# Gates by seven products: where the low parts, the second branch weights and the first output units are parted

## The chip, the cores and the metric

The kernel runs on one core of a Trainium2 chip. The metric is device time of one execution in microseconds (us). The kernel before takes 2453.77 us, the median of three runs (2452.86 to 2455.67).

## The reference

Two layers work on 512 tokens of width 1024, in fp32. Each layer is a SwiGLU feed-forward, a token mixer and a second feed-forward, each followed by a layer norm with a scaled residual. The mixer has three attention branches, `o_a`, `o_b` and `o_c`, each 512 x 512. The change lies in how they are merged:

```python
g = jax.nn.sigmoid(h @ w_gate + b_gate).reshape(B, S, N_BRANCH, D)
merged = g[:, :, 0] * (o_a @ w_br_a) + g[:, :, 1] * (o_b @ w_br_b) + g[:, :, 2] * (o_c @ w_br_c)
return merged @ w_out
```

`h` is 512 x 1024, `w_gate` 1024 x 3072, each `w_br` 512 x 1024 and `w_out` 1024 x 1024.

## The kernel before, in words

**Parts.** TensorE (PE) multiplies in fp32r, and each fp32 operand is split in two parts for it: the high part is a copy made by ScalarE (ACT), the low part is the operand less its high part, made by VectorE (DVE). A product is three matmuls, high by high, high by low and low by high, so the third matmul of a group needs the low part of the weights (`mm3`, L176; `prod`, L1643). `parts` (L1558) issues both halves of a split, ACT's and right behind it DVE's.

**Units and pairs.** The 1024 columns of each branch are eight units of 128. The merged value of branch `br` and unit `d` is a gate (`h` by `w_gate`, contraction 1024) times a branch value (`o` by `w_br`, contraction 512). The first units are made plainly: `plain` (L1657) takes 24 matmuls of 512 columns for a gate. The others are made in pairs of units `d` and `d + 1`, by seven block products for eight: `Two` (L1622) holds the weights of the pair (`rg`, `ru`), `sums` makes four block sums of them on DVE, and `hi` parts four operands: `ug`, `u1`, `u2` and `ud`. `token_sums` (L1602) makes the four sums of token blocks that all pairs share, in two halves `g`; each half is two additions (`back`) and four steps `both`: a subtraction on DVE, a high part on ACT and a low part on DVE.

**The cycle.** `cycle` (L1682) does one pair, the current one (`cur`), while it prepares the next (`nxt`). PE's order in it is seven products of 12 matmuls of 256 columns: two into bank `ga`, two into `pa`, one into `pb`, and two more into `ga`. ACT copies `ga` to `sn` after the second (L1691), and products six and seven then add onto `ga`: the sixth has to wait until `sn` is read. DVE adds the quarters up (L1696 to L1709), ACT makes two gate values by Tanh (L1708 and `gate_ev`, L1462). Behind the seven products come the branch units of the pair, 24 matmuls of 512 columns (`branch`, L1664), whose results DVE multiplies with the gates and adds up in `acc`.

**Order of the cycles.** The pairs are (1,6), (2,2), (2,4), (2,6), (0,2), (0,4) and (0,6). Two of them do two branches, and are called double here: (2,2) does the branch units (2,0) and (2,2), (0,2) does (0,0) and (0,2). They also begin with the split of the next attention output (`split_o`, L1562; its low part is the tile `ol`). Before the first cycle stand eight plain gates and branches, between which the token sums are dealt out two steps at a time (`some`, L1723).

**What sets the order.** The stage is inside `in_order` (L256): PE, ACT, DVE and GpSimd run in the order in which the code issues their instructions. Only the DMA queue of SyncE (SP) is ordered by the planner.

**Buffers.** Raw weights go through three buffers (`wraw`, L126, `raws` at L116). A buffer is free again when both halves of the split have read it. `raw_of` (L1570) loads 512 KB of gate weights with one DMA (L1573), `branch_w` (L1582) 512 KB of branch weights with two (L1586). A pair holds two of the three buffers, `rg` until the low part of `ug`, `ru` until the low part of `ud` (the tile `dl`). The loads for the pair after the next are issued as soon as buffers come free. In a double cycle the second branch's weights are parted into tile `wo`, in the loop at the end of the cycle (L1713), after everything for the next pair but `u2`.

**After the cycles.** `merged` parts the first six units of `acc` in the last cycle, the last two follow (L1766), and `rows_ln` (L287) does the output projection: for each 128 rows of `w_out` a load (`wrows`), a split (L161, L162) and 24 matmuls (L195 to L197) into all eight PSUM banks.

Of the kernel before, what the change touches and what calls it, by code (L numbers as in the profile page):

```python
# [9 lines left out]
F32 = mybir.dt.float32  # L10
F32R = mybir.dt.float32r
BF = mybir.dt.bfloat16
AF = mybir.ActivationFunctionType
OP = mybir.AluOpType
# [4 lines left out]
P = 128  # L19
S, D, F = 512, 1024, 2816  # L20
KD, KF, NB = D // P, F // P, S // P
# [43 lines left out]
def body(tc, a, out, depth=DEPTH):  # L65
    nc = tc.nc
# [7 lines left out]
    wt = pool("wt")  # L74
# [6 lines left out]
    def ps(tag=None, name="ps", shape=(P, 512)):  # L81
        if tag is None:
            tag = PS_ALL[ring[0] % 8]
            ring[0] += 1
        return psp.tile(list(shape), F32, name=name, tag=tag, bufs=PS_TAGS[tag])
# [40 lines left out]
    def wraw():  # L126
        pl, n = raws[0]
        raws.rotate(-1)
        return pl.tile([P, KD, P], F32, name="raw", tag="raw", bufs=n)

    more = K()
# [152 lines left out]
            load(when.pop(0))  # L284
        return wts, {0: lambda: ln.second(NB - 2), 2: lambda: ln.second(NB - 1)}

    def rows_ln(nk, wload, sh, sl, ln, nmain, clear, nxt):  # L287

        accs = [[ps(name="acc") for _ in range(2)] for _ in range(NB)]
        order = in_order()
        for k in range(nmain):
            w = wload(k)
            for tb in range(NB):
                mm_rows(accs, sh, sl, k, tb, w, nk)
        rest = [(k, wload(k)) for k in range(nmain, nk)]
        clear()
        nx.pool = pool("nx", reuse_waits="tile")

        def half(tb, hf):
            for k, w in rest:
                mm_rows(accs, sh, sl, k, tb, w, nk, (hf,))

        wts, pend = norm_tail(accs, half, ln, nxt)
        order.__exit__(None, None, None)
        return wts, pend
# [532 lines left out]
    def mix(l, wts, pend, done_ffn, xap, xa, nxt):  # L840
# [620 lines left out]
        def gate_ev(t, p, br, d):  # L1461
            nc.scalar.activation(t, p, AF.Tanh, scale=0.5, bias=bg[:, br, d:d + 1])  # L1462
# [92 lines left out]
            gate_ev(g1[br], held[br], br, 1)  # L1555
        order = in_order()

        def parts(hi, lo, x):  # L1558
            nc.scalar.activation(hi, x, AF.Copy)
            tt(lo, x, hi.bitcast(F32), op=OP.subtract)  # L1560

        def split_o(br, n=2):  # L1562
            for k in range(0, 4, n):
                c = slice(k, k + n)
                parts(ob[0][:, c], ob[1][:, c], o_t[br][:, c])

        def pair_of(pl):
            return [pl.tile([P, KD, P], F32R, name=n, tag=n, bufs=3 if pl is wt else 2) for n in ("hi", "lo")]
# [10 lines left out]
            parts(*u, r)  # L1579
            return u  # L1580

        def branch_w(br, d, pl):  # L1582
            r = wraw()
            v = wb[br].rearrange("(k p) f -> p k f", p=P)
            for j in range(2):
                nc.sync.dma_start(r[:, 4 * j:4 * j + 4], v[:, :, (d + j) * P:(d + j + 1) * P])  # L1586
            if pl is op:
                u = op.tile([P, 2, KD, P], F32R, name="wo", tag="o2")
                u = u[:, 0], u[:, 1]
            else:  # L1590
                u = pair_of(pl)
            parts(*u, r)
            return u

        def tick(t):
            sums_step(t[:, 0:1] if len(t.shape) == 2 else t[:, 0, 0:1])
# [4 lines left out]

        def token_sums(g):  # L1602
            x = op.tile([P, 4, S], F32, name="x", tag="o1")
            steps = []

            def back(i):
                c, o = slice(4 * i + 2 * g, 4 * i + 2 * g + 2), slice(2 * i, 2 * i + 2)
                tt(x[:, o], xh[:, c].bitcast(F32), xl[:, c].bitcast(F32), op=OP.add)

            p_, q, r_, s_ = x[:, 0:2, H1], x[:, 0:2, H2], x[:, 2:4, H1], x[:, 2:4, H2]  # L1610

            def both(i, o, u, v):
                tt(o, u, v, op=OP.subtract)
                c = slice(2 * g, 2 * g + 2)
                parts(T[i][0][:, c], T[i][1][:, c], o)

            steps += [lambda i=i: back(i) for i in range(2)]
            for z in ((0, p_, q, p_), (2, q, s_, q), (1, s_, s_, p_), (3, r_, r_, s_)):
                steps.append(lambda z=z: both(*z))
            return steps  # L1620

        class Two:  # L1622

# [13 lines left out]
            def hi(u, n):  # L1637
                x = {"ug": u.rg, "u1": u.x1, "u2": u.x2, "ud": u.ru[:, hi4]}[n] if n != "ug" else u.rg
                t = gd if n == "ud" else pair_of(more.pool if n == "ug" else wt)
                setattr(u, n, t)  # L1640
                parts(*t, x)

        def prod(o, w, k0, x, first=True):  # L1643
            for k in range(4):
                hi, lo = w[0][:, k0 + k], w[1][:, k0 + k]
                vh, vl = x[0][:, k], x[1][:, k]
                for i, (wx, vx) in enumerate(((hi, vh), (hi, vl), (lo, vh))):
                    nc.tensor.matmul(o, wx, vx, start=first and k == 0 and i == 0, stop=k == 3 and i == 2,  # L1648
                                     skip_group_check=True)
# [14 lines left out]
        def branch(br, d, w, mid=None):  # L1664
            for j in range(2):
                p = ps(name="brp")
                for k in range(4):
                    mm3(p, w, 4 * j + k, ob[0][:, k], ob[1][:, k], k == 0, k == 3)
                if mid and j == 0:
                    mid()  # L1670
                t, o = g[br, d + j], acc[:, d + j]
                if br == 1:
                    stt(o, t, 1.0, p, op0=OP.add, op1=OP.mult)
                else:
                    stt(t, t, 1.0, p, op0=OP.add, op1=OP.mult)
                    tt(o, o, t, op=OP.add)
            tick(o)
# [1 line left out]
        def temp(n):  # L1679
            return gp.tile([P, S], F32, name=n, tag=n, bufs=2)  # L1680

        def cycle(cur, nxt, brps, end=None):  # L1682
            ga, pa, pb = (ps(name="gate") for _ in range(3))
            if nxt:
                nxt.sums()
            br, d = brps[0]
            w = branch_w(br, d, wt)
            prod(ga[:, H1], cur.ug, 0, XP)
            prod(ga[:, H2], cur.u1, 0, T[0], False)
            sn, v, h = temp("sn"), temp("v"), gate_t(cur.br, cur.d + 1)  # L1690
            nc.scalar.activation(sn, ga, AF.Copy)  # L1691
            if nxt:
                nxt.hi("ug")
            prod(pa[:, H1], cur.u1, 4, T[1])
            prod(pa[:, H2], cur.u2, 0, T[2], False)
            tt(v[:, H1], pa[:, H1], sn[:, H1], op=OP.add)  # L1696
            tt(v[:, H2], pa[:, H2], v[:, H1], op=OP.add)
            tt(h[:, H2], sn[:, H2], v[:, H2], op=OP.add)
            if nxt:
                nxt.hi("u1")  # L1700
            prod(pb[:, H1], cur.ud, 0, T[3])
            tt(h[:, H1], pb[:, H1], v[:, H2], op=OP.add)
            prod(ga[:, H1], cur.ug, 4, XR, False)
            prod(ga[:, H2], cur.u2, 4, XS, False)
            if nxt:
                nxt.hi("ud")
            t = gate_t(cur.br, cur.d)
            nc.scalar.activation(h, h, AF.Tanh, scale=0.5, bias=bg[:, cur.br, cur.d + 1:cur.d + 2])  # L1708
            tt(ga[:, H2], ga[:, H2], v[:, H1], op=OP.add)  # L1709
            gate_ev(t, ga, cur.br, cur.d)  # L1710
            tick(t)
            mid = (lambda: nxt.hi("u2")) if nxt else end
            for i, (br, d) in enumerate(brps):  # L1713
                branch(br, d, w if i == 0 else branch_w(br, d, op), mid)
                mid = None

        wp = [gate_w(2, 1, wt)]
        split_o(1)
# [4 lines left out]
        def some(n):  # L1723
            for _ in range(n):
                steps.pop(0)()
# [17 lines left out]
        some(2)  # L1743
        plain(1, 5, wp[6])
        some(2)
        cur.sums()
        cur.hi("ug")
        branch(1, 4, wp[7])
        for n in ("u1", "u2", "ud"):
            cur.hi(n)  # L1750
        todo = deque([(2, 2), (2, 4), (2, 6), (0, 2), (0, 4), (0, 6)])
        then = Two(*todo.popleft())
        brps = {(1, 6): [(1, 6)], (2, 2): [(2, 0), (2, 2)], (0, 2): [(0, 0), (0, 2)]}

        def merged():
            for d in range(0, 6, 2):
                c = slice(d, d + 2)
                parts(mh[:, c], ml[:, c], acc[:, c])

        while cur:  # L1760
            me = cur.br, cur.d
            if me[1] == 2:
                split_o(me[0])
            cycle(cur, then, brps.get(me, [me]), merged)
            cur, then = then, Two(*todo.popleft()) if todo else None
        for d in (6, 7):  # L1766
            parts(mh[:, d], ml[:, d], acc[:, d])
        order.__exit__(None, None, None)
        gp.release()
        op.release()  # L1770
# [5 lines left out]
        for tb in range(NB):  # L1776
            nc.sync.dma_start(xa2[tb], x_sp[tb * P:(tb + 1) * P, :])
        wts, pend = rows_ln(KD, lambda k: wrows(a["w_out"][l], k), lambda k: mh[:, k], lambda k: ml[:, k], ln,
                            KD - NTAIL, lambda: None, nxt)

        def done():
            nx_close()
# [167 lines left out]
```

## Time and profile before

| What | us |
|---|---|
| median of three runs | 2453.77 |
| the profiled execution | 2453.74 |
| its span, first to last instruction | 2452.0 |
| PE busy | 2418.8 |
| DVE busy | 1947.3 |
| ACT busy | 1229.1 |

The mean granted clock of TensorE in the span is 0.996. The stage of the change stands twice in the span, once in each layer: its first cycle starts at 711.11 and at 1928.64 us, its output projection at 845.54 and at 2061.58 us.

How to read it: times in the rows are microseconds from the span's start. `lo<-raw,hi` is an instruction that writes a tile called `lo` from tiles called `raw` and `hi`; `x2` at the end says that two of them were merged in one row. In square brackets is the idle time of the engine just before, and the instruction that ended it. In the list of waits a row reads: engine, tile and line that waited, what ended the wait, microseconds in total, how often, and the longest. SPq is the DMA queue of SyncE. PEclk is the granted clock as a share of the full one. A matmul's row lasts longer than its share of PE, since the next one starts before it ends.

### The profile page before, as it was taken

How to read it: one execution, taken by the hardware profiler on the slowest of the kernel's cores; microseconds unless marked ns; L12 is line 12 of the kernel's file. 1: busy time of each engine (PE TensorE's matmuls, PEld its weight loads, DVE VectorE, ACT ScalarE, POOL GpSimd, SP SyncE). 2: the span in 40 equal slices, each digit the busy share in tenths (PEclk: the TensorE clock that was granted, in tenths of full speed). 3: DMA queues.
4: the chain of work that ended last, by engine and by line, in shares of the span. 5: the costliest groups of instructions: out<-in, count | busy, mean ns of one | idle time of the engine just before them, and what ended most of it. 6: DMA issues, size and time to landing. Idle time of an engine off the chain costs nothing.

```text
span 2452.0 us, 41947 instructions
## 1 busy us (share of the span) xinstructions
PE 2418.8 (99%) x15952; PEld 2160.7 (88%) x15952; DVE 1947.3 (79%) x3782; ACT 1229.1 (50%) x2336; POOL 487.8 (20%) x684
## 2 busy tenths in 40 slices
PE   9999999999999999999999999999999999999998
PEld 8999887888888889998899998878888888899987
DVE  6899976677677659999879999666776776699997
ACT  4445645576644334445534455456775443344463
POOL 4232402254410001124000004022443100000040
PEclk9999999999999999999999999999999999999999
DMA  7888753676463536787533347446655635333373
GB/s 205 230 223 219 251 170 118 175 166 142 113 180 86 182 119 155 206 208 237 189 110 104 104 139 243 144 141 173 168 134 132 156 95 172 104 95 104 105 242 121
DMA packets 422587, 390.09 MB, mean 159 GB/s; under 512 B 20473, under 2 KB 352393, under 8 KB 422385
## 3 DMA queue, kind: packets, MB, share of 16 engines
q1 hardware_dynamic: 385792, 287.00, 39.4%
q0 software_dynamic: 36592, 100.41, 17.1%
q8 instruction: 126, 2.06, 0.3%
q14 instruction: 77, 0.62, 0.1%
HBM read 360.02 MB, written 93.38 MB: 185 GB/s over the span
## 4 chain that ended last, share of the span: by engine, by line
PE 93%; DVE 4%; issue 1%; ACT 1%; DMA 1%; SPq 0%; DVEq 0%; POOLq 0%; ACTq 0%; POOL 0%
PE acc L331 17%; PE pg L647 17%; PE pu L647 8%; PE pj L182 6%; PE pj L183 6%; PE pj L184 6%; PE pv L647 4%; PE gate L1648 3%; PE sN L1258 2%; PE ptN L1300 1%; PE po L1319 1%; PE brp L184 1%; PE acc L195 1%; PE brp L183 1%; PE brp L182 1%; PE acc L197 1%
## 5 line engine op out<-in xcount | busy, mean ns | idle before, releaser
L162 DVE TENSOR_TENSOR lo<-raw,hi 128x1024 fp32r<-128x1024 f32 (+2 forms) x192 | 223.8, 1183 | 95.9 <-ACT hi L161 95.2
L182 PE MATMUL pj<-xh,hi 128*128 128x512 f32 (+1 forms) x720 | 267.0, 371 | 0.6 <-ACT hi L161 0.6
L161 ACT ACTIVATE hi<-raw 128x1024 fp32r<-128x1024 f32 (+2 forms) x192 | 192.1, 1020 | 130.0 <-PE acc L331 54.6
L184 PE MATMUL pj<-xh,lo 128*128 128x512 f32 (+1 forms) x720 | 254.6, 354 | 0.4 <-DVE lo L162 0.4
L183 PE MATMUL pj<-xl,hi 128*128 128x512 f32 (+1 forms) x720 | 254.4, 353 | 0.0
L647 PE MATMUL pg<-xh,lo 128*128 128x256 f32 x864 | 244.5, 283 | 0.0
L647 PE MATMUL pg<-xl,hi 128*128 128x256 f32 x864 | 244.5, 283 | 0.0
L647 PE MATMUL pg<-xh,hi 128*128 128x256 f32 x864 | 244.5, 283 | 0.0
L331 PE MATMUL acc<-hi,sh 128*128 128x512 f32 x568 | 221.5, 390 | 0.0
L331 PE MATMUL acc<-lo,sh 128*128 128x512 f32 x568 | 221.1, 389 | 0.0
L331 PE MATMUL acc<-hi,sl 128*128 128x512 f32 x568 | 221.0, 389 | 0.0
L352 POOL COPY pace<-sh 64x1 f32<-64x1 f32 x16 | 94.7, 5920 | 473.4 <-ACT sh L592 473.4
L544 DVE TENSOR_TENSOR lo<-ws,hi 128x1024 fp32r<-128x1024 f32 x144 | 175.2, 1217 | 0.0
L647 PEld LDWEIGHTS pg<-xh,hi 128*128 128x128 f32 x864 | 165.9, 192 | 0.2
L647 PEld LDWEIGHTS pg<-xl,hi 128*128 128x128 f32 x864 | 165.9, 192 | 0.2
L647 PEld LDWEIGHTS pg<-xh,lo 128*128 128x128 f32 x864 | 165.9, 192 | 0.0
L647 PE MATMUL pu<-th,hi 128*128 128x256 f32 x576 | 163.0, 283 | 0.0
L647 PE MATMUL pu<-tl,hi 128*128 128x256 f32 x576 | 163.0, 283 | 0.0
L647 PE MATMUL pu<-th,lo 128*128 128x256 f32 x576 | 163.0, 283 | 0.0
L184 PEld LDWEIGHTS pj<-xh,lo 128*128 128x128 f32 x720 | 136.1, 189 | 20.2 <-DVE lo L162 0.6
L541 ACT ACTIVATE hi<-ws 128x1024 fp32r<-128x1024 f32 x144 | 144.0, 1048 | 16.9 <-DVE ws L526 15.3
L182 PEld LDWEIGHTS pj<-xh,hi 128*128 128x128 f32 x720 | 136.4, 189 | 16.3 <-issue 3.7
(418 smaller groups left out, 7068.0 us busy)
## 6 DMA issues: line engine op xcount, KB each, us to landing
raw<-in_ffn_w_dram SPq DMA_DIRECT2D x228, 512.0 KB, 4.6
ts<-in_ffn_w_dram POOLq DMA_DIRECT2D x72, 768.0 KB, 7.5
raw<-in_w_in_dram SPq DMA_DIRECT2D x56, 512.0 KB, 4.0
raw<-ts SPq DMA_DIRECT2D x52, 512.0 KB, 3.9
raw<-in_w_gate_dram SPq DMA_DIRECT2D x48, 512.0 KB, 4.8
ts<-ts POOLq DMA_DIRECT2D x24, 768.0 KB, 7.8
x_sp<-xa POOLq DMA_DIRECT2D x24, 512.0 KB, 6.2
ks<-hl SPq DMA_DIRECT2D x96, 128.0 KB, 2.4
```

What stands on the lines that cost most here:

```text
L161: nc.scalar.activation(hi[:, c], raw[:, c], AF.Copy)
L162: nc.vector.tensor_tensor(lo[:, c], raw[:, c], hi[:, c].bitcast(F32), op=OP.subtract)
L182: nc.tensor.matmul(o, hi[:, k], vh, start=first, stop=False)
L183: nc.tensor.matmul(o, hi[:, k], vl, start=False, stop=False)
L184: nc.tensor.matmul(o, lo[:, k], vh, start=False, stop=last)
L331: nc.tensor.matmul(o, xx[:, t], ww[:, c], start=first and i == 0, stop=last and i == 2)
L352: nc.gpsimd.tensor_copy(pace[0:64], sp(min(p + 1, NS - 1))[0][0:64, 0, 0:1].bitcast(F32))
L541: nc.scalar.activation(t[0], x, AF.Copy)
L544: nc.vector.tensor_tensor(t[1], x, t[0].bitcast(F32), op=OP.subtract)
L647: nc.tensor.matmul(o, wx, vx, start=first and k == 0 and i == 0, stop=k == 3 and i == 2, skip_group_check=True)
L1258: nc.tensor.matmul(o[:, 0:nb].rearrange("p k b j -> p (k b j)"), q, kx[:, 2 * b0:2 * (b0 + nb)].rearrange("p a b -> p (a b)"), start=i == ...
L1648: nc.tensor.matmul(o, wx, vx, start=first and k == 0 and i == 0, stop=k == 3 and i == 2, skip_group_check=True)
```

## The change

Splits are issued in two steps. A new helper `high` issues ACT's half and returns a function that issues DVE's half later. `parts` is the two together. With it:

- In `token_sums`, the low part of each step is issued one step later, after the next subtraction. A half has seven steps for six, and one more `some(2)` stands before the first pair.
- The first pair's four high parts are issued together, then its four low parts, and the branch (1,4) behind them.
- In `cycle`, the weights of all its branches are loaded and their high parts issued at the head, ahead of `ug` and `sn`. The low parts follow `sn`. The high parts of `ug`, `u1`, `ud` and `u2` are issued one product sooner than their low parts; `u2` stands ahead of the second gate value.
- In the last cycle, the first unit of `w_out` is loaded and parted at the head, the high parts of the first six units of `acc` ahead of the gate value and their low parts behind it. Units 1 and 2 of `w_out` are parted right after the last branch, and `rows_ln` takes these three as `ready`.

```diff
-    def rows_ln(nk, wload, sh, sl, ln, nmain, clear, nxt):
+    def rows_ln(nk, wload, sh, sl, ln, nmain, clear, nxt, ready=()):
...
-            w = wload(k)
+            w = ready[k] if k < len(ready) else wload(k)
...
+        def high(hi, lo, x):
+            nc.scalar.activation(hi, x, AF.Copy)
+            return lambda: tt(lo, x, hi.bitcast(F32), op=OP.subtract)
+
         def parts(hi, lo, x):
-            nc.scalar.activation(hi, x, AF.Copy)
-            tt(lo, x, hi.bitcast(F32), op=OP.subtract)
+            high(hi, lo, x)()
...
-        def branch_w(br, d, pl):
+        def branch_w(br, d, pl, now=True):
...
-            parts(*u, r)
+            lo = high(*u, r)
+            if not now:
+                return u, lo
+            lo()
             return u
...
-                parts(T[i][0][:, c], T[i][1][:, c], o)
+                los.append(high(T[i][0][:, c], T[i][1][:, c], o))
+                if len(los) > 1:
+                    los.pop(0)()
...
-            return steps
+            return steps + [lambda: los.pop(0)()]
...
-                parts(*t, x)
+                return high(*t, x)
...
-        def cycle(cur, nxt, brps, end=None):
+        def cycle(cur, nxt, brps, end):
             ga, pa, pb = (ps(name="gate") for _ in range(3))
+            none = lambda: None
+            hi = nxt.hi if nxt else lambda n: none
             if nxt:
                 nxt.sums()
-            br, d = brps[0]
-            w = branch_w(br, d, wt)
+            ws = [branch_w(br, d, op if i else wt, False) for i, (br, d) in enumerate(brps)]
+            lo = hi("ug")
             prod(ga[:, H1], cur.ug, 0, XP)
             prod(ga[:, H2], cur.u1, 0, T[0], False)
             sn, v, h = temp("sn"), temp("v"), gate_t(cur.br, cur.d + 1)
             nc.scalar.activation(sn, ga, AF.Copy)
-            if nxt:
-                nxt.hi("ug")
+            for _, f in ws:
+                f()
+            lo()
             prod(pa[:, H1], cur.u1, 4, T[1])
+            lo = hi("u1")
             prod(pa[:, H2], cur.u2, 0, T[2], False)
...
-            if nxt:
-                nxt.hi("u1")
+            lo()
             prod(pb[:, H1], cur.ud, 0, T[3])
+            lo = hi("ud")
             tt(h[:, H1], pb[:, H1], v[:, H2], op=OP.add)
             prod(ga[:, H1], cur.ug, 4, XR, False)
+            lo()
+            nc.scalar.activation(h, h, AF.Tanh, scale=0.5, bias=bg[:, cur.br, cur.d + 1:cur.d + 2])
             prod(ga[:, H2], cur.u2, 4, XS, False)
-            if nxt:
-                nxt.hi("ud")
             t = gate_t(cur.br, cur.d)
-            nc.scalar.activation(h, h, AF.Tanh, scale=0.5, bias=bg[:, cur.br, cur.d + 1:cur.d + 2])
+            lo = hi("u2") if nxt else end()
             tt(ga[:, H2], ga[:, H2], v[:, H1], op=OP.add)
             gate_ev(t, ga, cur.br, cur.d)
+            lo()
             tick(t)
-            mid = (lambda: nxt.hi("u2")) if nxt else end
-            for i, (br, d) in enumerate(brps):
-                branch(br, d, w if i == 0 else branch_w(br, d, op), mid)
-                mid = None
+            for (br, d), (w, _) in zip(brps, ws):
+                branch(br, d, w)
...
         some(2)
+        some(2)
         cur.sums()
-        cur.hi("ug")
+        los = [cur.hi(n) for n in ("ug", "u1", "u2", "ud")]
+        for f in los:
+            f()
         branch(1, 4, wp[7])
-        for n in ("u1", "u2", "ud"):
-            cur.hi(n)
...
+        def out_w(k):
+            r = wraw()
+            nc.sync.dma_start(r.rearrange("p k f -> p (k f)"), wo[k * P:(k + 1) * P, :])
+            u = pair_of(wt if k else more.pool)
+            ws_.append(u)
+            return high(*u, r)
+
         def merged():
-            for d in range(0, 6, 2):
-                c = slice(d, d + 2)
-                parts(mh[:, c], ml[:, c], acc[:, c])
+            los = [high(mh[:, c], ml[:, c], acc[:, c]) for c in (slice(d, d + 2) for d in range(0, 6, 2))]
+            return lambda: [f() for f in los]
...
+            if not then:
+                out_w(0)()
             cycle(cur, then, brps.get(me, [me]), merged)
             cur, then = then, Two(*todo.popleft()) if todo else None
+        los = [out_w(k) for k in (1, 2)]
         for d in (6, 7):
-            parts(mh[:, d], ml[:, d], acc[:, d])
+            los.append(high(mh[:, d], ml[:, d], acc[:, d]))
+        for f in los:
+            f()
+        more.n = 3
```

More of the change, by code (lines that the diff above doesn't have):

```diff
@@ L1603, in token_sums @@
             x = op.tile([P, 4, S], F32, name="x", tag="o1")
-            steps = []
+            steps, los = [], []
             def back(i):
@@ L1753, in mix @@
         brps = {(1, 6): [(1, 6)], (2, 2): [(2, 0), (2, 2)], (0, 2): [(0, 0), (0, 2)]}
+        wo, ws_ = a["w_out"][l], []
+        def out_w(k):
[4 more added lines that the diff above has]
+            return high(*u, r)
         def merged():
-            for d in range(0, 6, 2):
-                c = slice(d, d + 2)
-                parts(mh[:, c], ml[:, c], acc[:, c])
+            los = [high(mh[:, c], ml[:, c], acc[:, c]) for c in (slice(d, d + 2) for d in range(0, 6, 2))]
+            return lambda: [f() for f in los]
         while cur:
@@ L1778, in mix @@
         wts, pend = rows_ln(KD, lambda k: wrows(a["w_out"][l], k), lambda k: mh[:, k], lambda k: ml[:, k], ln,
-                            KD - NTAIL, lambda: None, nxt)
+                            KD - NTAIL, lambda: None, nxt, ws_)
         def done():
```

## The prediction

> **What bounds the kernel now.** I read the page first. The profiled execution took 2453.74 us, of which its span is 2452.0; the other 1.74 us lie outside and I keep them. The runs shown have the median 2453.77, so a sum made on the profiled execution may be read as one on the median.
>
> ```profile
> PE 2418.8 (99%) x15952; PEld 2160.7 (88%) x15952; DVE 1947.3 (79%) x3782; ACT 1229.1 (50%) x2336; POOL 487.8 (20%) x684
> ```
>
> TensorE is the bound, and the change removes and adds no matmul. It can only move the time in which PE stands still. So the second view is the list of waits, for PE alone:
>
> ```profile
> PE brp L184 <- DVE wo L1560: 12.0, 4, 3.0
> PE gate L1648 <- DVE lo L1560: 4.9, 3, 2.1
> PE gate L1648 <- ACT sn L1691: 1.8, 2, 1.3
> ...
> PE acc L195 <- DVE t L1675: 0.7, 2, 0.4
> ```
>
> These rows of both layers are what the change can reach: 12.0 + 4.9 + 1.8 + 0.7 = 19.4 us. Third, the windows view puts a price on each place, since a wait also costs what follows it. The columns are the stretch, its length, five engines with their busy time, the granted clock, the share of DMA, GB/s.
>
> ```profile
> core 0: us, PE busy (x) PEld busy (x) DVE busy (x) ACT busy (x) POOL busy (x), PEclk, DMA share, GB/s
> 711.11:726.00 14.89, 10.85 (x85) 10.23 (x84) 12.26 (x17) 6.59 (x8) 0.00 (x0) 1.00 0.32 93
> 731.47:741.54 10.07, 10.07 (x85) 10.07 (x84) 9.90 (x15) 5.37 (x7) 0.00 (x0) 1.00 0.14 42
> 726.00:731.47 5.47, 5.47 (x26) 4.51 (x25) 3.63 (x6) 3.18 (x4) 0.00 (x0) 1.00 0.79 230
> 741.54:757.47 15.93, 12.89 (x50) 10.11 (x49) 8.69 (x12) 4.37 (x5) 0.00 (x0) 0.89 0.39 110
> 798.63:814.47 15.84, 12.89 (x51) 10.12 (x50) 8.60 (x12) 4.37 (x5) 0.00 (x0) 0.89 0.38 110
> 1928.64:1943.59 14.95, 12.28 (x85) 11.59 (x84) 12.26 (x17) 6.59 (x8) 0.00 (x0) 0.89 0.34 95
> 1959.13:1975.06 15.93, 12.89 (x51) 10.09 (x50) 8.70 (x12) 4.36 (x5) 0.00 (x0) 0.89 0.37 110
> 2016.20:2030.51 14.31, 11.36 (x51) 8.95 (x50) 8.60 (x12) 4.37 (x5) 0.00 (x0) 1.00 0.42 122
> 845.54:852.00 6.46, 6.03 (x26) 4.35 (x24) 6.42 (x9) 2.61 (x4) 0.00 (x0) 1.00 0.70 210
> ```
>
> An undisturbed set of seven products takes 10.07 us and an undisturbed branch of 24 matmuls 5.47. Against these, cycle (1,6) loses 14.89 - 10.07 = 4.82 and 14.95 - 10.07 = 4.88. The two double branches, (2,0) with (2,2) and (0,0) with (0,2), should take 10.94; they lose 4.99, 4.90, 4.99 and 3.37, together 18.25. The last of these four ran at clock 1.00, the others at 0.89: a half-clock stretch behind the wait costs 4.96 (their mean) - 3.37 = 1.6 us. The first unit of the output projection loses 6.46 - 5.47 = 1.0, in each layer. All other cycles have no gap (731.47:741.54 is busy throughout), so what the change does in them is worth nothing unless it breaks them.
>
> **The second branch weights, moved to the head of the double cycles.** This is the largest term, and I take it from the queues. ACT and DVE work in the order in which the kernel is written, and three raw buffers are all there are. At the head of cycle (0,2) two of them hold the gate weights of the next pair, the third the weights of (0,0). The second branch's load needs a buffer; the rows show when it gets one (DVE, then the SP queue, then the landings of all branch loads of the first layer's cycles), what ACT does meanwhile, and when the sixth product starts on PE:
>
> ```profile
> 792.12 1.05 ACT L1559 ACTIVATE hi<-raw 128x1024 fp32r<-128x1024 f32 x1
> ```
> ```profile
> 794.89 2.35 DVE L1560 TENSOR_TENSOR lo<-raw,hi 128x1024 fp32r<-128x1024 f32 x2
> ```
> ```profile
> 796.14 0.92 SPq L1586 DMA_DIRECT2D raw<-in_w_br_a_dram  x2
> ```
> ```profile
> DMA to landing us min/median/max: 2.7/3.3/4.9
> ```
> ```profile
> 795.75 0.28 PE L1648 MATMUL gate<-xh,hi 128*128 128x256 f32 x1
> ```
>
> The load is issued at 796.14, just when the first of the two low parts of 794.89 (half of 2.35) is done. That frees the buffer of (0,0). The change does not free it earlier: its low part still stands behind the four sums on DVE. What changes is who waits. Today ACT parts `ug` at 792.12 and the second weights only after `u2`, at the end of the cycle, long after they have landed. In the new order the high part of the second weights stands ahead of `ug` and of `sn` on ACT. So ACT must wait for the load: second half issued at about 796.6 (half of 0.92 later), landing 3.3 after that at 799.9; high part 0.97 (721.43 to 722.40 in the rows below), 800.85; `ug`, 801.8; `sn`, 0.58, 802.4. The sixth product writes on the bank that `sn` reads and was due at 795.75. It starts 0.05 after that: a wait of about 6.7 us. What is queued behind on ACT is everything else of the cycle, and DVE waits as well, since the low part of the second weights stands ahead of that of `ug`.
>
> That this is how the queues behave is shown in cycle (1,6) of before, where the same thing happens on a smaller scale:
>
> ```profile
> 721.43 1.06 ACT L1559 ACTIVATE hi<-raw 128x1024 fp32r<-128x1024 f32 x1 [7.31 <-DMA raw<-in_w_br_b_dram]
> 722.40 0.58 ACT L1691 ACTIVATE sn<-gate 128x512 f32<-128x512 f32 x1
> ```
> ```profile
> 723.03 0.39 PE L1648 MATMUL gate<-xh,hi 128*128 128x256 f32 x1 [1.27 <-ACT sn L1691]
> ```
>
> A high part waits 7.31 us for its load, `sn` runs right behind it, and PE resumes 0.05 after `sn`.
>
> Cycle (2,2) is the same with one shift. Here DVE comes to the head late today:
>
> ```profile
> 730.68 1.23 DVE L1560 TENSOR_TENSOR lo<-ws,hi 128x1024 fp32r<-128x1024 f32 x1 [1.76 <-ACT hi L1559]
> 731.82 1.28 DVE L1673 SCALAR_TENSOR_TENSOR acc<-t,brp 128x512 f32<-128x512 f32 x2
> 733.02 2.36 DVE L1560 TENSOR_TENSOR ol<-o,oh 128x1024 fp32r<-128x1024 f32 x2
> ```
>
> With the low part of `u2` moved ahead of the branch, the last accumulation can start some 0.2 after PE leaves the branch at 731.47 (an estimate: PE's last matmul ends after the next has started) and take half of 1.28. The `ol` row moves from 733.02 to about 732.3, and the whole chain by 0.7: a wait of 6.0.
>
> To each wait I add what row 2016.20 shows beyond the bare wait (3.37 against 3.0, so 0.4) and one half-clock stretch (1.6). That is 6.0 + 6.7 + 2 x 2.0 = 16.7 per layer, 33.4 in both. The four waits for `wo` end, since its low part is done long before the second branch; they gave 18.25. Net +15.15 us. The landing is the open size: 2.7 or 4.9 instead of 3.3 make it 2.4 less or 6.4 more over four cycles; I take the median, since no gate load will run beside it.
>
> [...]
>
> **Cycle (1,6).** Product one waits for the low part of `ug`. Its chain starts when ACT has evacuated gate (1,5) and runs through the last token sum:
>
> ```profile
> 707.11 0.69 DVE L1560 TENSOR_TENSOR mm<-x,mm 128x512 fp32r<-128x512 f32 x1 [2.15 <-ACT mm L1559]
> 707.72 0.69 DVE L1613 TENSOR_TENSOR x<-x 128x512 f32<-128x512 f32 x1
> 709.10 0.69 DVE L1560 TENSOR_TENSOR mm<-x,mm 128x512 fp32r<-128x512 f32 x1 [0.70 <-ACT mm L1559]
> ```
>
> One step behind means that three high parts, not two, follow the evacuation. DVE then does a low part at 707.11, the last sum at 707.72, the low part that was put off at 708.33, and the last one when its high part is there, at 709.10 as today. The 0.7 us hole is filled with work that used to lie earlier. `ug` and product one gain nothing.
>
> The four low parts of the first pair then stand together, the two accumulations of branch (1,4) behind them; that is 1.2 us sooner for `u1` and `ud`.
>
> ```profile
> 715.98 0.39 PE L1648 MATMUL gate<-mm,lo 128*128 128x256 f32 x1 [0.63 <-DVE lo L1560]
> ...
> 721.48 0.28 PE L1648 MATMUL gate<-mm,dl 128*128 128x256 f32 x1
> ```
> ```profile
> 716.97 0.69 DVE L1560 TENSOR_TENSOR dl<-raw,dh 128x512 fp32r<-128x512 f32 x1
> ```
> ```profile
> 717.69 0.92 SPq L1586 DMA_DIRECT2D raw<-in_w_br_b_dram  x2
> ```
>
> The wait of 0.63 (0.9 with the restart, an estimate) goes. But PE only comes to product six sooner, at 720.7 for 721.6, and that one waits for `sn`. The branch load is issued once `dl` has freed a buffer, so 1.2 us sooner; the high part of `ug`, now ahead of `sn`, takes 0.95 of it back. Product six starts 0.25 sooner: 0.5 us in both layers. Its wait grows to about 2.1, the length at which one of today's two (14.89 at clock 1.00, 14.95 at 0.89) had a half-clock stretch. Before, that stretch was hidden under the next wait; now nothing is behind it. Bounds 0 and 2 x 1.6; I take one, +1.6.
>
> **The last cycle.**
>
> ```profile
> 851.20 0.50 PE L195 MATMUL acc<-hi,mm 128*128 128x512 f32 x1 [0.36 <-DVE t L1675]
> ```
> ```profile
> 840.20 2.96 ACT L161 ACTIVATE hi<-raw 128x1024 fp32r<-128x1024 f32 x3 [0.68 <-ACT hi L161]
> 843.06 0.67 ACT L1462 ACTIVATE t<-gate,bgate 128x512 f32<-128x512 f32 x1
> ```
>
> Today units of the output weights are parted ahead of the last gate value, three of them just before it, so that it comes at 843.06, and their low parts keep DVE from the last branch's result, for which the output projection then waits. In the new order unit 0 is parted at the head of the cycle, where DVE is free of pair sums, and units 1 and 2 after the branch; unit 1 is wanted 5.4 us later. The 1.0 us per layer goes: -2.0, bounds 0 and -2.0. Unit 0's load stands ahead of the last branch's on SP, which then goes out one buffer release later, 1.2 us (half of 2.35); loads for a single cycle go out most of a cycle before they are wanted, so that covers it.
>
> **Edits at nothing.** In single cycles the low parts are issued one step later and `u2` before the gate value: DVE no longer waits for ACT (1.76 in the row at 730.68), but PE has no gap there. The gate value comes 0.97 later and is wanted only when PE ends the first branch unit, 2.7 after product seven. The next pair's loads slip by about 5 us in a double cycle; they are wanted a whole cycle later. POOL's copies and weight sums feed the next stage.
>
> **Sum.** +15.15 - 0.5 + 1.6 - 2.0 = +14.25 on 2453.74: 2468.0. Lowest: short landings (-2.4), no clock loss in (1,6) (-1.6), and half-clock stretches of which half falls into the wait (-0.8 x 4): 2460.8. Highest: long landings, 2474.4.
>
> **Rivals.** First, the intended outcome, and faster: the second weights have landed when ACT comes to them. The four waits of 18.25 go without a new one, with -0.5 and -2.0: 2433. It decides if the load is issued 3.8 us (0.46 + 3.3) before 792.12, where ACT now goes on after the first weights, so by 788.3. For it speaks that the first branch's load is always early. Against it stands the SP queue, which holds the second load back for the low part of the first:
>
> ```profile
> SPq L1586 <- DVE lo L1560: 8.0, 1, 8.0
> ```
>
> It would need a fourth buffer, or another order on ACT than the written one; chance 0.10. Second, no change that can be measured: the new waits are there but come without clock loss and with landings of 2.7. That is 5.4 + 6.1 + 0.8 per layer, 24.6 for 18.25, less 2.5: +3.85, 2457.6. Half-clock stretches followed three waits of about 3 us out of four, and these are twice as long: 0.10. Third, a longer half clock. Row 741.54 lacks 0.11 of the clock in 15.93 us, so some 3.5 us ran at half. A wait of over 6 us is longer than such a stretch; the clock would be halved within it, and if PE's return in the middle of a stretch does not count, a second one follows, at up to 3.2 for 1.6 each time. With all four: 2468.0 + 6.4 = 2474.4. 0.12. [...] The forecast keeps 0.68.
>
> **How the numbers follow.** About 0.2% (4.9 us) is what a measurement of this kernel can tell from no change. Forecast and third rival lie above +0.2%: slower 0.80. Second: same 0.10. First: faster 0.10. The range 2454 to 2474.5 holds the forecast's 2460.8 to 2474.4, the third up to its full price and the upper part of the second; it leaves out the first and the tails.
>
> **What would show it.** Right: in the waits of PE, `brp <- DVE wo` is gone, and `gate <- ACT sn` has grown from 1.8 to about 2 x (6.0 + 6.7) plus 2 x 2.1 us; in ACT, a high part in both double cycles that waits 7 to 9 us for a branch load, `ug` and `sn` behind it; SP issuing the second load right after the first low part; the 2.1 before product one unchanged; no wait for `t` at L1675 under the output projection. Wrong: the second load issued before that low part, or `sn` at 3 us into the double cycles as now; then the first rival holds. If the waits are there and the time is lower than forecast, the clock column of the double cycles tells it.

## The result and the profile after

The changed kernel takes 2468.93 us (median of six runs, 2467.5 to 2470.85) against 2453.37 for the kernel before in the same session (2452.86 to 2455.67). The ratio is 1.0062, 95% interval 1.0049 to 1.0075: slower by 0.6%, with 2468.0 forecast. The profiled execution took 2468.07, its span is 2466.4.

The engines' line of the page, and below it the waits of PE (total, times, longest):

```profile
PE 2423.0 (98%) x15952; PEld 2168.5 (88%) x15952; DVE 1949.1 (79%) x3782; ACT 1228.2 (50%) x2336; POOL 487.4 (20%) x684
```
```profile
PE gate L1656 <- ACT sn L1701: 25.1, 6, 6.6
PE gate L1656 <- DVE lo L1560: 4.3, 2, 2.1
```

The number of matmuls is the same. `brp <- DVE wo` (12.0) and `acc <- DVE t` (0.7) are gone from the list, and the wait for `sn` has gone from 1.8 to 25.1 us. The windows view prices it; the rows are cycle (1,6), then products and branches of the double cycles (2,2) and (0,2), then the first output unit, in the first layer and in the second:

```profile
710.61:725.18 14.57, 12.06 (x85) 11.65 (x84) 13.33 (x19) 6.59 (x8) 0.00 (x0) 0.88 0.42 118
1935.93:1950.41 14.48, 12.08 (x86) 11.67 (x84) 13.33 (x19) 6.59 (x8) 0.00 (x0) 0.88 0.41 116
730.65:748.48 17.83, 12.05 (x85) 11.85 (x84) 12.21 (x16) 6.68 (x8) 0.00 (x0) 0.81 0.30 87
748.48:759.57 11.09, 11.09 (x51) 9.03 (x50) 5.80 (x8) 3.65 (x4) 0.00 (x0) 1.00 0.18 51
790.65:809.55 18.90, 12.34 (x85) 12.13 (x84) 12.89 (x17) 6.68 (x8) 0.00 (x0) 0.82 0.29 82
809.55:820.63 11.08, 11.08 (x51) 9.03 (x50) 5.80 (x8) 3.65 (x4) 0.00 (x0) 1.00 0.17 50
1955.88:1973.84 17.96, 12.07 (x86) 11.87 (x85) 12.20 (x16) 6.68 (x8) 0.00 (x0) 0.81 0.28 84
2016.00:2034.77 18.77, 12.49 (x86) 12.28 (x85) 12.90 (x17) 6.69 (x8) 0.00 (x0) 0.82 0.29 84
851.71:857.15 5.44, 5.44 (x25) 4.50 (x24) 5.37 (x8) 2.30 (x3) 0.00 (x0) 1.00 0.47 140
2076.94:2082.38 5.44, 5.44 (x25) 4.50 (x24) 5.37 (x8) 2.29 (x3) 0.00 (x0) 1.00 0.47 131
```

Seven undisturbed products take 10.07 us, so the products of the four double cycles lose 7.76, 8.83, 7.89 and 8.70, and each double branch 0.14: 33.7 us for the 18.25 of before. Cycle (1,6) loses 0.8 less than before in the two layers together, the first output unit 2.0 less. That makes +15.5 - 0.8 - 2.0 = +12.7 of the 14.4 by which the span has grown.

In cycle (0,2) the cause stands in four queues, DVE, SP, ACT and PE:

```profile
796.99 1.22 DVE L1560 TENSOR_TENSOR lo<-raw,hi 128x1024 fp32r<-128x1024 f32 x1
```
```profile
798.23 0.92 SPq L1589 DMA_DIRECT2D raw<-in_w_br_a_dram  x2
```
```profile
802.03 1.06 ACT L1559 ACTIVATE wo<-raw 128x1024 fp32r<-128x1024 f32 x1 [9.16 <-DMA raw<-in_w_br_a_dram]
802.99 1.04 ACT L1559 ACTIVATE hi<-raw 128x1024 fp32r<-128x1024 f32 x1
803.93 0.58 ACT L1701 ACTIVATE sn<-gate 128x512 f32<-128x512 f32 x1
```
```profile
804.57 0.58 PE L1656 MATMUL gate<-xh,hi 128*128 128x256 f32 x1 [6.56 <-ACT sn L1701]
```

The low part of the first branch weights ends at 798.2 and frees the third buffer; the load goes out at once, 7.58 us into the cycle, as in the kernel before (796.14 - 788.56). ACT waits 9.16 us for it with `ug` and `sn` behind, and PE waits for `sn`.

### The profile page after: what moved, and what is told of

Same layout as the page of the kernel before. It is cut to its first block, busy times and chain, and to the rows that moved or that the text cites. A ratio compares the mean times of both kernels' runs of the same rounds, so it can differ in the third digit from the quotient of the medians.

```text
span 2466.4 us, 41973 instructions
## 1 busy us (share of the span) xinstructions
PE 2423.0 (98%) x15952; PEld 2168.5 (88%) x15952; DVE 1949.1 (79%) x3782; ACT 1228.2 (50%) x2336; POOL 487.4 (20%) x684
## 4 chain that ended last, share of the span: by engine, by line
PE 96%; DVE 2%; DMA 1%; ACT 1%; issue 1%; POOL 0%; SPq 0%; DVEq 0%; POOLq 0%; ACTq 0%
PE acc L331 17%; PE pg L647 17%; PE pu L647 8%; PE pj L182 6%; PE pj L183 6%; PE pj L184 5%; PE gate L1656 5%; PE pv L647 4%; PE brp L184 2%; PE brp L182 2%; PE brp L183 2%; PE sN L1258 2%; PE ptN L1300 1%; PE po L1319 1%; PE acc L196 1%; PE acc L197 1%
## 5 line engine op out<-in xcount | busy, mean ns | idle before, releaser
L162 DVE TENSOR_TENSOR lo<-raw,hi 128x1024 fp32r<-128x1024 f32 (+2 forms) x186 | 217.2, 1186 | 88.9 <-ACT hi L161 87.9
L161 ACT ACTIVATE hi<-raw 128x1024 fp32r<-128x1024 f32 (+2 forms) x186 | 185.8, 1019 | 131.3 <-PE acc L331 52.9
```

The costliest lines, as they stand in the source:

```text
L161: nc.scalar.activation(hi[:, c], raw[:, c], AF.Copy)
L162: nc.vector.tensor_tensor(lo[:, c], raw[:, c], hi[:, c].bitcast(F32), op=OP.subtract)
```

## The experiments

Each time is a median with the ratio to the kernel before from the same session, in which that took 2453.0 to 2454.1.

**The second branch weights back at the loop's end.**

```diff
-            ws = [branch_w(br, d, op if i else wt, False) for i, (br, d) in enumerate(brps)]
+            ws = [branch_w(*brps[0], wt, False)]
...
-            for (br, d), (w, _) in zip(brps, ws):
-                branch(br, d, w)
+            for i, (br, d) in enumerate(brps):
+                branch(br, d, branch_w(br, d, op) if i else ws[0][0])
```

> The kernel after, with one part undone: the second branch weights of the double cycles are loaded and parted in the loop at the cycle's end again. Theory (the order on ACT at the head of the double cycles costs the time): the four waits of product six for sn of 6 to 6.7 us go, the four waits for wo of 3.0 come back, and what the rest of the change gains stays, 2.5 us: 2451 us, 1.5 either way. Rival (the other edits cost it, by disturbing the single cycles or cycle (1,6)): at least half of the 15 us stays, 2461 to 2469.

Measured 2443.18 us, ratio 0.9956 (0.9942 to 0.9970): 26 us faster than the kernel after, and 8 us better than the theory's number. The four waits for `wo` came back, but shorter, and without any loss of clock (waits of PE; then the first double branch):

```profile
PE brp L184 <- DVE wo L1560: 8.7, 4, 2.2
```
```profile
741.28:754.81 13.53, 11.35 (x50) 8.95 (x49) 8.04 (x12) 4.71 (x6) 0.00 (x0) 1.00 0.41 116
```

All four take 13.5, at clock 1.00, a loss of 2.6 each: 10.4 for 18.25. DVE shows why. In the kernel before the second weights are parted behind all four parts of the next pair, `u2` too. The low part of `u2` comes late there, and the four accumulating steps stand in a row between it and the low part of `wo` (three of them shown), for which PE waits:

```profile
745.62 1.23 DVE L1560 TENSOR_TENSOR lo<-ws,hi 128x1024 fp32r<-128x1024 f32 x1 [1.70 <-ACT hi L1559]
746.76 0.68 DVE L1675 SCALAR_TENSOR_TENSOR g<-g,brp 128x512 f32<-128x512 f32 x1
747.47 0.69 DVE L1676 TENSOR_TENSOR acc<-acc,g 128x512 f32<-128x512 f32 x1
748.08 0.68 DVE L1675 SCALAR_TENSOR_TENSOR g<-g,brp 128x512 f32<-128x512 f32 x1
...
749.41 1.22 DVE L1560 TENSOR_TENSOR wo<-raw,wo 128x1024 fp32r<-128x1024 f32 x1
```

In this experiment it comes 0.86 after the gate sum, DVE has caught up, and is itself waiting when PE ends the second unit:

```profile
743.76 1.22 DVE L1560 TENSOR_TENSOR lo<-ws,hi 128x1024 fp32r<-128x1024 f32 x1 [0.86 <-ACT hi L1559]
...
746.95 0.69 DVE L1683 SCALAR_TENSOR_TENSOR g<-g,brp 128x512 f32<-128x512 f32 x1 [0.64 <-PE brp L184]
...
748.28 1.22 DVE L1560 TENSOR_TENSOR wo<-raw,wo 128x1024 fp32r<-128x1024 f32 x1
```

From the end of the products (741.54 before, 741.28 here) to the low part of `wo` it is 7.9 us before and 7.0 here.

So the rest of the change is worth more than the 2.5 us that the prediction gave it, and the place of the second weights costs 26.

**The order within the cycle, alone.** In the kernel before: high parts one product ahead of their low parts (so `ug` ahead of `sn`), the low part of the first branch weights behind `sn`, `u2` ahead of the gate value, and nothing else of the change. Its last lines:

```diff
...
+            lo = hi("u2")
             tt(ga[:, H2], ga[:, H2], v[:, H1], op=OP.add)
             gate_ev(t, ga, cur.br, cur.d)
+            lo()
             tick(t)
-            mid = (lambda: nxt.hi("u2")) if nxt else end
...
```

> The kernel before, with one part of the change alone: the order of the high and low parts within a cycle (one product sooner, u2 ahead of the gate value). Second branch weights, token sums, first pair and output units are as before. Theory from the run with the second weights at the loop's end: the four waits for wo fall from 3.1 to 2.3 us because the low part of u2 no longer stands between the accumulations, and fewer half-clock stretches follow: 7.5 us less, 2446.5 us, 2444 to 2450. Rival, the prediction's own sum (this order is worth nothing as long as the wait for wo stands): 2453 to 2455.

Measured 2448.99 us, 0.9983 (0.9975 to 0.9992). The waits for `wo` are 8.7 in all, as above, and the branches 13.53 again, 7.9 us less. But cycle (1,6) got longer, 16.01 and 17.13 for 14.89 and 14.95, which takes 3.3 back:

```profile
1924.45:1941.58 17.13, 12.24 (x85) 11.63 (x84) 14.65 (x21) 7.16 (x9) 0.00 (x0) 0.90 0.42 120
```

So the order is worth 4 us by itself. With the token sums and the first pair as in the change, (1,6) takes 14.5 to 14.7 (the experiment above and the kernel after), and the 3.3 us are not lost; which of these two edits does it was not separated.

**The head of the cycle, alone.** The kernel before, with only the prediction's main term:

```diff
-            br, d = brps[0]
-            w = branch_w(br, d, wt)
+            ws = [branch_w(br, d, op if i else wt) for i, (br, d) in enumerate(brps)]
...
-                branch(br, d, w if i == 0 else branch_w(br, d, op), mid)
+                branch(br, d, ws[i], mid)
```

> The kernel before, with one part of the change alone: the weights of both branches of a double cycle loaded and parted at its head. Theory, the main term of the prediction: the four waits for wo go (18.25 us) and four waits for sn come; ug stands behind sn here, so each is 0.95 shorter than in the kernel after, and DVE comes 0.7 later to the head of cycle (2,2): 5.7 us each and 2.0 for restart and clock, 31 us. Net +12.5: 2466 us, 2463 to 2469. Rival (without the other edits the load lands in time, or the waits hide each other): within 3 us of the kernel before, 2450 to 2456.

Measured 2467.44 us, 1.0057 (1.0044 to 1.0069). Nearly the whole loss is in this one edit, 14.0 us of 15.6. The waits of PE for `sn`:

```profile
PE gate L1648 <- ACT sn L1690: 23.4, 6, 5.6
```

**A fourth buffer.** The kernel after, with the second weights loaded into two gate tiles that are free by then, each half parted by itself:

```diff
+        def second_w(br, d):
+            v = wb[br].rearrange("(k p) f -> p k f", p=P)
+            u = op.tile([P, 2, KD, P], F32R, name="wo", tag="o2")
+            los = []
+            for j, r in enumerate((g1[1], gates0[1])):
+                r = r.rearrange("p (k f) -> p k f", k=4)
+                nc.sync.dma_start(r, v[:, :, (d + j) * P:(d + j + 1) * P])
+                los.append(high(u[:, 0, 4 * j:4 * j + 4], u[:, 1, 4 * j:4 * j + 4], r))
+            return (u[:, 0], u[:, 1]), lambda: [f() for f in los]
...
-            ws = [branch_w(br, d, op if i else wt, False) for i, (br, d) in enumerate(brps)]
+            ws = [second_w(br, d) if i else branch_w(br, d, wt, False) for i, (br, d) in enumerate(brps)]
```

> The kernel after, with the second branch weights loaded into two tiles that are free by then, so that the load does not wait for the low part of the first branch weights; the place on ACT at the head of the cycle stays. The two halves are parted one by one, two instructions more on ACT and on DVE in each double cycle. Theory (ACT waits because the load is issued only when a raw buffer is free): PE's four waits for sn in the double cycles fall to under 1 us, no wait for wo comes, 2435 us, 2432 to 2440. Rival (the four high and low parts at the head are too much work for ACT and DVE, wherever the load is): the waits stay above 3 us each and the time above 2455.

Measured 2435.11 us, 0.9922 (0.9910 to 0.9935). The order on ACT is that of the kernel after; only the load no longer waits for a buffer, and in cycle (0,2) nothing on ACT waits for it:

```profile
785.67 1.14 ACT L1559 ACTIVATE wo<-g 128x512 fp32r<-128x512 f32 x2
786.71 1.05 ACT L1559 ACTIVATE hi<-raw 128x1024 fp32r<-128x1024 f32 x1
787.66 0.57 ACT L1711 ACTIVATE sn<-gate 128x512 f32<-128x512 f32 x1
```

The work at the head is not too much for ACT and DVE; the buffer was what held it.

**`sn` first.** The kernel after with one line moved; the load is as late as before:

```diff
-            ws = [branch_w(br, d, op if i else wt, False) for i, (br, d) in enumerate(brps)]
+            ws = [branch_w(*brps[0], wt, False)]
...
             nc.scalar.activation(sn, ga, AF.Copy)
+            ws += [branch_w(br, d, op, False) for br, d in brps[1:]]
```

> The kernel after, with one line moved: load and high part of the second branch weights are issued right behind sn, not ahead of ug and sn. The load goes out as late as before and ACT still waits for it, but sn no longer stands behind it. Theory (the time is lost because PE's product six hangs on sn): no wait for sn in the double cycles, the rest of the cycle on DVE and ACT comes 5 to 6 us late and is just in time for the next cycle: 2434 us, 2432 to 2438. Rival (the late load delays the gates and the next pair all the same): a wait of 2 us or more turns up at the branches or at the next cycle's first products, 2442 or more.

Measured 2433.77 us, 0.9920 (0.9906 to 0.9934). ACT still stands still for 6.79 us in cycle (2,2), now behind `sn`, and PE does not notice (ACT; then the seven products of (2,2)):

```profile
734.14 0.60 ACT L1701 ACTIVATE sn<-gate 128x512 f32<-128x512 f32 x1
741.52 1.06 ACT L1559 ACTIVATE wo<-raw 128x1024 fp32r<-128x1024 f32 x1 [6.79 <-DMA raw<-in_w_br_c_dram]
```
```profile
731.07:741.14 10.07, 10.07 (x85) 10.07 (x84) 6.59 (x8) 3.47 (x4) 0.00 (x0) 1.00 0.19 54
```

So the late load costs nothing in itself. What costs is that the one instruction for which PE waits stands behind it.

**The second weights behind `u2` and the gate value.** No extra buffer, load and parts just ahead of the first branch:

```diff
-            ws = [branch_w(br, d, op if i else wt, False) for i, (br, d) in enumerate(brps)]
+            ws = [branch_w(*brps[0], wt, False)]
...
             gate_ev(t, ga, cur.br, cur.d)
+            late = [branch_w(br, d, op, False) for br, d in brps[1:]]
             lo()
+            for _, f in late:
+                f()
             tick(t)
-            for (br, d), (w, _) in zip(brps, ws):
+            for (br, d), (w, _) in zip(brps, ws + late):
```

> The kernel after, with load and high part of the second branch weights issued after u2 and the gate value, and the low part behind that of u2, ahead of the first branch; no extra buffer. Theory (only the place on ACT and DVE matters): sn comes at its old time, the low part of wo is done before the first branch is half through, so neither wait is there: 2433 us, 2430 to 2438. Rival (a second branch's weights can't be ready in the cycle without waiting, the load or the low part is late wherever it stands): waits for wo of 2 us or more stay in the double cycles, 2445 to 2455.

Measured 2433.87 us, 0.9918 (0.9904 to 0.9931); in the double cycles neither wait is there. Its two cycles (1,6) show something else, one with a half-clock stretch and one without (clock 0.88 and 1.00):

```profile
711.00:725.54 14.54, 12.07 (x85) 11.66 (x84) 13.38 (x19) 6.59 (x8) 0.00 (x0) 0.88 0.43 119
1917.16:1931.72 14.56, 10.57 (x85) 10.16 (x84) 13.32 (x19) 6.59 (x8) 0.00 (x0) 1.00 0.43 120
```

They take the same time. The slower PE only comes later to product six, which has to wait for `sn` anyway: 0.4 us in the first, 1.8 us in the second.

**The wait filled with work.** The kernel after, with 24 matmuls more in each double cycle, ahead of product six:

```diff
+            if len(brps) > 1:
+                dm = ps(name="gate")
+                for i in range(24):
+                    nc.tensor.matmul(dm, cur.ug[0][:, i % 8], xh[:, i % 8], start=i == 0, stop=i == 23)
             prod(ga[:, H1], cur.ug, 4, XR, False)
```

> The kernel after, with 24 extra matmuls of 512 columns (128 x 512, 24 x 0.23 = 5.4 us, their result is not used) on PE ahead of product six in the double cycles: PE is busy in most of the wait for sn, and product six starts when it would have. Theory (the wait costs its own length, and a half clock behind it about 1.6 to 2.0 us more): product six starts no later, the clock stays at 1.00 in the double cycles, so 4 x 1.7 us less: 2462 us, 2460 to 2464. Rival (the clock takes no part, the wait is all): no change, 2468 to 2470.

Measured 2460.96 us, 1.0033 (1.0021 to 1.0044): 96 matmuls more, 8 us less. The products of (0,2) take 16.83 with the extra work, 18.90 without:

```profile
788.75:805.58 16.83, 15.80 (x109) 14.49 (x108) 11.64 (x15) 5.96 (x7) 0.00 (x0) 1.00 0.22 65
```

The other three double cycles gain 1.8, 1.9 and 1.7; all four have clock 1.00, for 0.81 to 0.82 in the kernel after. Product six starts within 0.2 us of its place in the kernel after in three of the four and 0.5 later in the fourth; from there to the branch PE takes 3.0 us for 4.7 to 5.1. So these 7.5 us of 33.7 are the clock's share of the loss.

**The first output units, alone**, in the kernel before:

```diff
+            if not then:
+                out_w(0)()
...
+        los = [out_w(k) for k in (1, 2)]
```

> The kernel before, with one part of the change alone: the first three units of the output weights parted in and right behind the last cycle. Theory: the wait for the last branch's result ahead of the output projection goes, 1.0 us in each layer: 2451.8 us, 2450.5 to 2453.5. Rival (the wait only moves, to unit 1 or to the last units of acc): 2453.8, within 1 us of the kernel before.

Measured 2450.63 us, 0.9990 (0.9981 to 0.9999). The first output unit takes 5.44 for 6.46 in both layers; the further 1.4 us are within the interval.

```profile
843.87:849.31 5.44, 5.44 (x25) 4.50 (x24) 5.37 (x7) 3.56 (x5) 0.00 (x0) 1.00 0.00 0
```

**The first pair ahead of gate (1,5).** The experiment with the second weights behind `u2`, and besides:

```diff
-        plain(1, 5, wp[6])
         some(2)
         some(2)
         cur.sums()
         los = [cur.hi(n) for n in ("ug", "u1", "u2", "ud")]
         for f in los:
             f()
+        plain(1, 5, wp[6])
         branch(1, 4, wp[7])
```

> The kernel with the second weights behind u2 and the gate value (2433.9 us), and besides the last four token-sum steps and the whole preparation of the first pair issued ahead of the gate unit (1,5), so that ACT and DVE do not wait for its evacuation first. Theory (both waits of cycle (1,6) hang on that evacuation, by which ACT stands idle for 4.2 us): product one no longer waits 2.1 us, the branch load goes out some 4 us sooner and sn is not late, 4.5 us in each layer: 2425 us, 2424 to 2428. Rival (the first pair is limited by the work of DVE or by its loads): at least half of the waits stays, 2429 to 2434.

Measured 2425.30 us (four runs, 2424.24 to 2432.18), 0.9894 (0.9879 to 0.9910), the fastest version of all: 27.7 us below the kernel before. ACT parts `ug` in the time in which it used to wait for gate (1,5), and evacuates that gate later; cycle (1,6) then loses 0.6 us in the first layer and 0.5 in the second (ACT; windows):

```profile
704.49 1.05 ACT L1559 ACTIVATE hi<-raw 128x1024 fp32r<-128x1024 f32 x1
...
709.54 0.67 ACT L1462 ACTIVATE t<-gate,bgate 128x512 f32<-128x512 f32 x1
```
```profile
710.85:721.55 10.70, 10.33 (x85) 10.12 (x84) 9.19 (x14) 3.96 (x5) 0.00 (x0) 1.00 0.52 149
```

## Why the prediction was right, and where only by luck

- **Main term: right in cause and size.** 33.7 us of loss for 33.4 forecast, net +15.5 for +15.15. The bare waits were 5.78, 6.56, 5.89 and 6.28 us, 24.5 in all for the 25.4 forecast, and what comes on top was 9.2 for 8.0; that the sum fits so closely is partly luck. The load goes out at the very place, it lands 3.3 us after its second half (798.69 to 802.03), and by itself the edit costs 14 us. The first rival, the intended outcome at 2433, needed "a fourth buffer, or another order on ACT"; with each of the two the kernel takes 2435.1 and 2433.8.
- **The clock's share in it: right in size, wrong in kind.** One half-clock stretch of 3.4 us per wait was forecast, at 1.6. In the profile of after each wait comes with two, 6.8 us together (from 740.89, 802.33, 1966.28 and 2027.72), as the third rival had it, but 1.9 to 2.9 us of the 6.8 lie inside the wait, where they cost nothing. Filling the waits gave 1.65 to 2.07 each, where the forecast had 1.6 for the clock (2.0 with the 0.4 beyond the bare wait).
- **Cycle (1,6): the step that failed.** "Before, that stretch was hidden under the next wait; now nothing is behind it", +1.6. In the profiled run it was still hidden: half-clock stretches in both layers (clock 0.88) and yet 0.8 us less than before. The stretch follows the wait of 2.1 us before product one (in the first layer the wait ends at 713.14 and the half clock begins at 713.59, in the second at 1938.47 and 1938.97). So PE came later to product six, and the wait for `sn`, forecast at 2.1, was 0.4 and 0.3: no second stretch came behind it. The experiment with the second weights behind `u2` has the cycle at 14.54 with the stretch and 14.56 without. A half clock behind the wait for `sn` itself came in the second layer of the filled-wait experiment: after a wait of 1.97 us the matmuls of product six start 0.21 us apart, for 0.12 ahead of it, and the cycle takes 17.66 us at clock 0.81, for 14.48 at 0.88 in the kernel after. How much of these 3.2 us is the clock and how much a later `sn` was not separated. The cycle's own -0.5 measured -0.8.
- **The missing 1.7.** The stage is +12.7, the span +14.4. By the starts of the stages the time ahead of the first is 0.5 shorter, and that between the two 2.1 longer. The profile of after has a half-clock stretch at 1642 us, in the attention of the second layer, behind a wait for a DMA that the kernel before has as well (1.3 us, 1.2 there), but without a stretch (clock 1.00 from 1631.56 to 1638.39):

```profile
1638.60:1642.01 3.41, 2.01 (x11) 1.17 (x11) 0.76 (x2) 0.27 (x2) 0.00 (x0) 1.00 0.65 174
1642.01:1645.42 3.41, 3.41 (x12) 2.73 (x11) 1.59 (x12) 1.88 (x10) 0.00 (x0) 0.50 0.79 251
```

  Half of 3.41 is 1.7, an estimate of its cost. No edit touches that code. Why the stretch came was not shown: the two waits differ by 0.1 us. So the forecast was 1.6 too high in the stage, and a stretch outside it, whose cause stays open, made up for it: that is luck. Whether the other runs of after had the same stretch isn't known, since one of them was profiled.
- **The last cycle: right**, -2.0 for -2.0, in the change and alone.
- **"Edits at nothing": right for the change, wrong for the code.** The order within the cycle cuts the wait for `wo` from 3.0 to 2.2 us and takes its half-clock stretches away (clock 1.00 in all four branches, where three of the four in the kernel before have 0.89). Under this change it bought nothing, because that wait is not there. The prediction priced the order only where it fell together with the moved weights, and so held the rest of the change for worth 2.5 us when it is worth about 11.

## What to carry to other kernels

On an engine that works in written order, look for the instruction that another engine waits for, and put nothing ahead of it that can wait itself: the same load, as late, made 2468.9 us ahead of `sn` and 2433.8 behind it. "Load earlier" is an empty order as long as the buffer comes free at the same time; find the release, and count from there. And price a change's parts one by one: here the place of one line turned a gain of 20 us (with the load behind `sn`) into a loss of 15.

## What the runs showed of the hardware

In the traces of the kernels before and after, the granted clock of PE is 1.00 or 0.50, with nothing between. Apart from the end of the span, the kernel before has four stretches at 0.50, each 3.41 us long, from 750.92, 808.95, 1931.93 and 1969.48. The kernel after has three of that length, from 713.59, 1642.01 and 1938.97, and four of 6.8 us, from 740.89, 802.33, 1966.28 and 2027.72. Each began behind a wait of PE or within one. The same double branch, at its wait for `wo`, in the kernel before and in the experiment with the second weights at the loop's end:

```profile
747.51:750.92 3.41, 0.37 (x2) 0.24 (x2) 3.08 (x4) 0.00 (x0) 0.00 (x0) 1.00 0.00 0
750.92:754.33 3.41, 3.41 (x9) 2.64 (x9) 0.00 (x0) 0.06 (x1) 0.00 (x0) 0.50 0.51 154
```
```profile
744.76:748.17 3.41, 2.62 (x12) 1.83 (x10) 2.71 (x5) 0.50 (x1) 0.00 (x0) 1.00 0.31 92
748.17:751.59 3.42, 2.03 (x9) 1.67 (x10) 1.33 (x2) 0.00 (x0) 0.00 (x0) 1.00 0.21 62
```

The first wait, 3.0 us, ended at 750.68, and the clock was 0.50 from 750.92. The second was 2.2 us long, with 0.8 us idle in the first row and 1.4 in the second, and the clock stayed at 1.00 in both rows and over the whole branch. In the kernel before, three of the four waits for `wo` (2.95 to 3.04 us) were followed by such a stretch, and none of eight of 2.2 us in the experiments with the order alone and with the weights at the loop's end (clock 1.00 in all eight branches). The waits of 2.14 us before product one of cycle (1,6), though, were followed by one in both layers of the kernel after and in the second layer of the kernel before, and not in the first layer there (clock 1.00). So the length of the wait alone does not tell these cases apart, and what does was not shown.

At each of the four waits of 5.78 to 6.56 us in the kernel after, the clock fell to 0.50 within the wait and stayed there for 6.8 us (here cycle (0,2), a wait of 6.56 us that ended at 804.57):

```profile
798.92:802.33 3.41, 0.00 (x0) 0.00 (x0) 0.00 (x0) 0.30 (x1) 0.00 (x0) 1.00 0.53 154
802.33:805.74 3.41, 1.17 (x5) 1.18 (x6) 2.62 (x3) 3.41 (x5) 0.00 (x0) 0.50 0.04 13
805.74:809.16 3.42, 3.42 (x18) 3.42 (x17) 2.98 (x6) 0.96 (x2) 0.00 (x0) 0.50 0.97 276
```

In the attention of the second layer a wait of 1.31 us in the kernel after was followed by a stretch, and one of 1.20 us at the same place in the kernel before was not. The end of a matmul is modelled in the profile, so these idle times are not exact.
